# Expert stage of a three-block transformer step: PSUM banks by turns, one bias product for small experts, splits on one engine, another order of experts

## The chip, the cores and the metric

One core of a Trainium2 chip runs the whole program in one launch. The metric is the device time of that launch in microseconds (us); the median of three runs stands for the kernel.

## What is computed

Three transformer blocks follow one another on 512 tokens of width 1024. The change touches only the mixture of experts in the first block. Cut to what matters here:

```python
def moe(h, w_router, b_router, w1, b1, w2, b2):
    logits = xf @ w_router + b_router              # 512 tokens, 32 experts
    top_val, top_idx = lax.top_k(logits, 4)
    gates = jax.nn.softmax(top_val, axis=-1)
    ...
    def expert_block(xb, e):
        u = xb @ w1[e] + b1[e]                     # 1024 -> 2048
        glu = jnp.minimum(u[:, ::2], 7.0)
        lin = jnp.clip(u[:, 1::2], -7.0, 7.0)
        a = glu * jax.nn.sigmoid(1.702 * glu) * (lin + 1.0)
        return a @ w2[e] + b2[e]                   # 1024 -> 1024
    ...                                            # y[token] += gate * row
```

All arrays are 32-bit floats, so each expert has 12 MB of weights, and every expert is used.

## The kernel before

The program is written in a framework that takes instructions in program order, reorders them on each engine by a model of its own, assigns buffers from pools (a tag with `bufs=n` has n slots) and sets the semaphores. Each engine then works through its own queue in that fixed order. An instruction that waits holds up everything behind it on its engine.

Experts are ranked by their number of tokens. Rank 0 is expert F0. Ranks 1 and 2 ("heavy") have one block of 128 slots and one of 64; ranks 3 to 16 ("large") have one block of 128, 96 or 80 slots; ranks 17 to 31 ("small") have one block of 64. Below L9 is the large expert of rank 9, S24 the small one of rank 24, H1 and H2 the heavy ones. Tokens beyond that room would go through a loop at the end (L1410), which makes no pass with these inputs.

Each expert is one call of `expert` (L1228) with three products over 1024 rows, called gemms here: two halves of w1 (`hf` 0 and 1) and w2. A gemm takes four weight units of 1 MB, each with two of the eight k-tiles `kt`.

- **A large block** works in split precision. For each k-tile `wsplit` (L299) makes a rounded high part on ScalarE (L302) and the rest on VectorE (L303), or on GpSimd for the k-tiles that `on_pool` names, which is `kt` 3 of every gemm. Then six products of 512 columns follow (L1260). Three slots exist for each part, and every fourth split takes another pair (`vh`, `vl`).
- **A small block** multiplies the unsplit weights in full 32-bit form. Its two column halves lie in the upper and the lower 64 partitions of one PSUM bank and run side by side.

Each gemm starts with its bias, added by a product of a selector (`sel`) with the table `bias` (L1246). The table's rows come in four groups of 32: high parts and rests of the first 1536 of 3072 columns, then those of the last 1536. A small block needs two such products per gemm, one of them in full 32-bit form; the trace shows three records for the two.

After each half of w1 the gate is computed from PSUM (L1273 to L1277: VectorE, with a tanh on ScalarE), and TensorE transposes the result (L1207) into the operand of w2. After w2 ScalarE scales the rows (L1322, L1325) and GpSimd adds them to the array `yd` in DRAM by an indirect DMA (L1323, L1326). The gather of a block's tokens (L1217, L1221) is a DMA of GpSimd's queue too.

Weight loads are issued by SyncE (L951, L296) into nine `mraw` and two `raw` buffers of 1 MB; a buffer is free again when its last reader is done. PSUM has eight banks: the tag `mm` has two slots of two banks, `s1` two of one bank, `t` two of one bank for transposes.

The order is fixed by hand (L1302 to L1312): F0 S17 L3 S18 L4 S19 L5 S20 L6 S21 H2 L7 S22 L8 S23 L9 S24 L10 S25 L11 H1 S26 L12 S27 L13 S28 L14 S29 L15 S30 L16 S31. Before the last expert, `collect` (L1328) reads `yd` back with four loads on SyncE's queue into two `mraw` buffers. Its eight `add` steps transpose that with TensorE (L1337) and add it to x (L1338); in program order they belong to the last expert's w2 gemm, where `gemm` takes two after each odd k-tile.

Of the kernel before, what the change touches and what calls it, by code (L numbers as in the profile page):

```python
# [11 lines left out]
F32 = mybir.dt.float32  # L12
# [912 lines left out]

N1 = 17
N2 = 2
HEAVY, SKIP = (5, 10), (4, 9)
ROOM = (128,) * 6 + (96,) * 4 + (80,) * 7 + (64,) * 15
OV = 32 + N2  # L930
NB = OV + 15
# [2 lines left out]
def moe(k):  # L934
# [27 lines left out]
    bias = mp.tile([128, 1536], F32R, name="bias")  # L962
    bf = mr.tile([128, 2048], F32, tag="mraw", name="bf", bufs=9)[:, 0:1536]
    for j in range(4):
        o_ = 1536 * (j // 2)
        nc.sync.dma_start(bf[32 * j:32 * j + 32], a["b12"][:, o_:o_ + 1536])
    S.activation(bias, bf, AF.Copy)
    for r_ in (slice(32, 64), slice(96, 128)):
        for c in range(2):
# [25 lines left out]
            S.activation(row[:, cc], ps, AF.Copy, scale=k.rc[:, t:t + 1])  # L995
        G.dma_start(hrow[t * 128:(t + 1) * 128], row, accum_op=ALU.add)
    yield
    k.psum(mm=2, s1=2, t=2)
    ep = es.enter_context(tc.tile_pool(name="ep", bufs=2))
    gd = ep.tile([128, 8, 32], F32, name="gd", bufs=1)  # L1000
    G.memset(gd, 1.0 / D)
# [39 lines left out]
    fl = lambda v: v.rearrange("p e t -> p (e t)")  # L1041
    V.tensor_tensor_scan(fl(Mi), fl(t4), fl(M), 0.0, op0=ALU.mult, op1=ALU.add)

    cnt, pg = (k.pt("s1") for j in range(2))
    nc.tensor.matmul(cnt[0:32, 256:320], Mi[:, :, 3], k.ones[:, 0:64], start=True, stop=True, skip_group_check=True)
    nc.tensor.matmul(cnt[:, 0:128], k.ones, fl(Mi), start=True, stop=True, skip_group_check=True)
    total = cnt[:, 0:128].rearrange("p (e t) -> p e t", t=4)[:, :, 3]
# [177 lines left out]
            X.append(at)  # L1225
        return X

    def expert(w1, w2, blocks, selcol, between=None, on_pool=((3,),) * 3, last=False, drain=False, to=lambda: None):  # L1228

        X = gather(blocks)
        A = [operand("a", False, lambda v, kt: v[:, kt // 4 * 2 + kt % 2, 64 * (kt % 4 // 2):64 * (kt % 4 // 2) + 64]) if b_[0] == 64
             else operand("a", True, lambda v, kt, ns=b_[0]: v[:, kt, 0:ns]) for b_ in blocks]
        split = any(b_[0] > 64 for b_ in blocks)

        def gemm(w, ops, bcol):

            pss = []
            for ns, *_ in blocks:  # L1240
                ps = k.pt("s1").unsqueeze(1) if ns == 64 else k.pt("mm", (128, 2, 512))
                o = [ps[64 * c:64 * c + 64, 0] if ns == 64 else ps[0:ns, c] for c in range(2)]
                for c in range(2):
                    hf, b0 = divmod(bcol + c * 512, 1536)
                    f = (lambda v: v.bitcast(F32)) if ns == 64 and c else (lambda v: v)
                    nc.tensor.matmul(o[c], f(selcol[:, hf]).to_broadcast([128, ns]), f(bias[:, b0:b0 + 512]), start=True, stop=False)  # L1246
                pss.append((ps, o))
            for q in range(4):
                raw = w[q]() if callable(w[q]) else w[q]
                for j in range(2):  # L1250
                    kt = 2 * q + j
                    if between and not last and bcol == 1024 and kt == 4:
                        between[0]()
                    if split:
                        hi, lo = ready.pop(0) if ready else wsplit(raw[:, j], kt in on_pool[bcol // 1024], to())
                    for op_, (_, o) in zip(ops, pss):
                        terms = ((op_[0], hi), (op_[0], lo), (op_[1], hi)) if len(op_) == 2 else ((op_[0], raw[:, j]),)
                        for n_, (l, r_) in enumerate(terms):
                            for c in range(2):
                                nc.tensor.matmul(o[c], l(kt), r_[:, c * 512:(c + 1) * 512], start=False,  # L1260
                                                 stop=kt == 7 and n_ == len(terms) - 1)
                    if adds and kt % 2 and (drain or not split):
                        adds.pop(0)()
                        if adds and not (split and len(blocks) == 1):
                            adds.pop(0)()
            return [ps if b_[0] == 64 else ps[0:b_[0]] for (ps, _), b_ in zip(pss, blocks)]
        for hf in range(2):
            for ps, (a_, _), (ns, *_) in zip(gemm([w1(hf, q) for q in range(4)], X, hf * 1024), A, blocks):
                w, nh = ps.shape[0:2]
                pg, pl = ps[:, :, 0:256], ps[:, :, 256:512]  # L1270
                tl = lambda name, bufs: ep.tile([128, 2, 256], F32, tag=name, name=name, bufs=bufs)[0:w, 0:nh]
                gl, th, ln = tl("gl", 2), tl("gt", 1), tl("ln", 1)
                V.tensor_scalar(gl, pg, 7.0, None, op0=ALU.min)  # L1273
                S.activation(th, gl, AF.Tanh, scale=0.5 * 1.702)  # L1274
                V.tensor_scalar(ln, pl, 7.0, -7.0, op0=ALU.min, op1=ALU.max)
                V.scalar_tensor_tensor(gl, th, 1.0, gl, op0=ALU.add, op1=ALU.mult)
                V.scalar_tensor_tensor(gl, ln, 1.0, gl, op0=ALU.add, op1=ALU.mult)  # L1277
                n = 2 * nh
                to_features([v[:, n * hf:n * hf + n] for v in a_], gl.rearrange("p a b -> p (a b)"), n, w, 0.5)
            if hf and between and not last:  # L1280
                between[1]()
        adds.extend(collected)
        collected.clear()
        pys = gemm([w2(q) for q in range(4)], [a_[1] for a_ in A], 2048)
        while adds and (drain or not split):
            adds.pop(0)()
        for py, (ns, _, tok, gcol, *row) in zip(pys, blocks):
            if not last:
                scatter(py, gcol, row[0], ns)
                continue  # L1290
            rows, *steps = add_rows(py, gcol, tok, ns, last)
            rows()
            adds.extend(steps)
        while last and adds:
            adds.pop(0)()
            if between and len(adds) == 0:
                between()
# [1 line left out]
    def block(b):  # L1299
        return (ROOM + (64,) * N2)[b], tabi[:, b:b + 1] if b else gi0, tab[:, 0, b:b + 1], tab[:, 1, b:b + 1], tabi[:, b:b + 1]  # L1300
    sq = lambda ap: ap.rearrange("o p a f -> p (o a) f")
    small, large = list(range(N1, 32)), list(range(1, N1))  # L1302

    for i_, x_ in zip(HEAVY, reversed(range(1, N2 + 1))):
        large.remove(x_)
        large.insert(i_, x_)
    order = [0, small.pop(0)]
    for i_, x_ in enumerate(large):
        order.append(x_)
        if i_ not in SKIP:  # L1310
            order.append(small.pop(0))
    assert sorted(order) == list(range(32))  # L1312
    k.sg = k.sm.tile([128, T], F32, tag="nwt", name="sg", bufs=1)

    yd, yd2 = k.yd, k.yd.rearrange("t (a b) -> (t a) b", a=2)
# [12 lines left out]
    def collect():  # L1328

        ys = [mr.tile([128, 2, D], F32, tag="mraw", name="yc", bufs=9) for j in range(2)]  # L1330
        for t in range(4):
            nc.sync.dma_start(ys[t // 2][:, t % 2], yd[128 * t:128 * t + 128])

        def add(n):
            ps = k.pt("mm", (128, 2, 512))[:, 0]
            for t in range(4):
                nc.tensor.transpose(ps[:, t * 128:(t + 1) * 128], ys[t // 2][:, t % 2, n * 128:(n + 1) * 128], k.ident)  # L1337
            V.scalar_tensor_tensor(k.x[:, n], ps, mod[:, 40 + n:41 + n], k.x[:, n], op0=ALU.mult, op1=ALU.add)  # L1338
        return [lambda n=n: add(n) for n in range(8)]

    def add_rows(py, gcol, tok, ns, last):
# [27 lines left out]
        def add(n):  # L1369
            if n == 0:  # L1370
                st["P"] = k.sm.tile([128, T], F32R, tag="tmp", name="Pm", bufs=3)
                for t in range(4):
                    V.tensor_scalar(st["P"][:, t * 128:(t + 1) * 128], iota, 1.0 + 128 * t, tok, op0=ALU.add, op1=ALU.is_equal)
            if n % 2 == 0:
                st["ps"] = k.pt("mm", (128, 2, 512))
            ps = st["ps"][:, n % 2]
            for i, (y, r_) in enumerate(st["y"]):
                nc.tensor.matmul(ps, y[r_, 128 * n:128 * n + 128], st["P"][r_], start=i == 0, stop=i == len(st["y"]) - 1)
            if last and st["prev"]:
                sums(*st["prev"])  # L1380
            V.scalar_tensor_tensor(k.x[:, n], ps, mod[:, 40 + n:41 + n], k.x[:, n], op0=ALU.mult, op1=ALU.add)
            if last:
                sq_ = k.sm.tile([128, T], F32, tag="tmp", name="sq", bufs=3)
                S.activation(sq_, k.x[:, n], AF.Square)
                st["prev"] = n, sq_
# [8 lines left out]
    for p in order:  # L1394
        blocks = [block(p)] + ([block(31 + p)] if 1 <= p <= N2 else [])
        if p == 0:
            expert(lambda hf, q: first[4 * hf + q], lambda q: (lambda: wload(a["w2"][0, q])), blocks, sel[:, :, 0:1], (tables, tables2), ((6,), (2, 4, 6), (3,)))
            prev = 0
            continue
        e = nc.values_load(sigi[0:1, p:p + 1], engines=(mybir.EngineType.SP,), min_val=0, max_val=31)  # L1400
        own = p == order[-1]
        drain = own
        prev = p
        if own:
            collected.extend(collect())
        expert(lambda hf, q: (lambda: wload(sq(a["w1"][bass.ds(e, 1), hf, q]), own)),
               lambda q: (lambda: wload(sq(a["w2"][bass.ds(e, 1), q]), own)), blocks, sel[:, :, p:p + 1], last=own, drain=drain,
               between=first_weights if own else None)
    nov = nc.values_load(ovi[0:1, 0:1], min_val=0, max_val=15)
    with tc.For_i(0, nov, 1) as i:  # L1410
# [894 lines left out]
```

## Time and profile before

| | |
|---|---|
| median of 3 runs | 3476.31 us (3474.74 to 3478.86) |
| profiled execution | 3469.57 us |
| its span, first to last instruction | 3467.8 us |
| TensorE busy | 3252.7 us, 94% |
| VectorE busy | 1955.9 us, 56% |
| ScalarE busy | 1337.4 us, 39% |
| GpSimd busy | 536.6 us, 15% |
| mean granted TensorE clock | 0.980 |

Busy shares are means over stages with different limits. PE is TensorE, PEld its weight loads, DVE VectorE, ACT ScalarE, POOL GpSimd, SP SyncE; a name with q is an engine's sequencer. In a row, the text in brackets is how long the engine sat idle before the instruction and what released it. The expert stage lies from 706.6 us to about 2007 us of the span.

### The profile page before, as it was taken

The numbers are of one execution on the slowest core, as the hardware profiler recorded it, in microseconds if no ns is written. First come the engines' busy times: TensorE is split into PE (matmuls) and PEld (weight loads), VectorE is DVE, ScalarE is ACT, GpSimd is POOL, SyncE is SP. The second block draws the span as 40 slices with busy tenths as digits, with TensorE's granted clock in tenths as the row PEclk, the third lists the DMA queues.
The fourth block names the chain that finished last, engine by engine and source line by source line (L and its number), as shares of the span: only waits on it lengthen the run. The fifth ranks groups of instructions, "written<-read, shape, count | busy, mean of one in ns | idle before, by whom it ended". The sixth has DMA issues, their size and how long they took to land. (4 is left out here: it accounts for less than half of the span.)

```text
span 3467.8 us, 41222 instructions
## 1 busy us (share of the span) xinstructions
PE 3252.7 (94%) x15711; PEld 2236.4 (64%) x15711; DVE 1955.9 (56%) x2879; ACT 1337.4 (39%) x1966; POOL 536.6 (15%) x546
## 2 busy tenths in 40 slices
PE   6999999979899998899988799999999999999998
PEld 6779887755554544444444366777777777678876
DVE  7651335474554644574445467765646765555655
ACT  2233344333443533454334245332224533344433
POOL 1223000231211111221112010221111011010001
PEclk9999999989999999999999899999999999999999
DMA  7437223559998799969999511444522210022222
GB/s 264 170 114 249 96 77 126 191 189 391 360 364 310 263 352 361 367 239 343 360 360 356 229 66 52 152 169 158 182 89 100 96 46 4 14 86 97 89 94 85
DMA packets 110425, 668.50 MB, mean 193 GB/s; under 512 B 14416, under 2 KB 14520, under 8 KB 41744
## 3 DMA queue, kind: packets, MB, share of 16 engines
q1 hardware_dynamic: 82272, 575.44, 43.1%
q0 software_dynamic: 27952, 90.38, 9.2%
q8 instruction: 125, 2.05, 0.2%
q14 instruction: 76, 0.62, 0.1%
HBM read 647.56 MB, written 28.63 MB: 195 GB/s over the span
## 5 line engine op out<-in xcount | busy, mean ns | idle before, releaser
L302 ACT ACTIVATE whi<-raw 128x1024 fp32r<-128x1024 f32 x344 | 362.9, 1058 | 664.9 <-PE mm L353 507.4
L303 DVE TENSOR_TENSOR wlo<-raw,whi 128x1024 fp32r<-128x1024 f32 x342 | 422.7, 1239 | 297.8 <-ACT whi L302 290.8
L352 PE MATMUL mm<-h_hi,whi 128*128 128x512 f32 x1440 | 576.4, 400 | 4.7 <-DVE th L637 1.6
L353 PE MATMUL mm<-h_lo,whi 128*128 128x512 f32 x1440 | 575.9, 400 | 0.0
L354 PE MATMUL mm<-h_hi,wlo 128*128 128x512 f32 x1440 | 574.8, 399 | 0.0
L303 DVE TENSOR_TENSOR wlo<-mraw,whi 128x1024 fp32r<-128x1024 f32 x256 | 331.8, 1315 | 114.4 <-ACT whi L302 111.4
L352 PEld LDWEIGHTS mm<-h_hi,whi 128*128 128x128 f32 x1440 | 270.6, 188 | 82.7 <-issue 13.2
L353 PEld LDWEIGHTS mm<-h_lo,whi 128*128 128x128 f32 x1440 | 270.7, 188 | 67.8 <-issue 7.0
L354 PEld LDWEIGHTS mm<-h_hi,wlo 128*128 128x128 f32 x1440 | 270.6, 188 | 67.4 <-issue 5.6
L302 ACT ACTIVATE whi<-mraw 128x1024 fp32r<-128x1024 f32 x258 | 268.7, 1054 | 86.7 <-PE mm L1260 60.6
L1260 PE MATMUL mm<-whi,x 128*80 128x512 f32 (+2 forms) x816 | 244.6, 403 | 0.0
L1260 PE MATMUL s<-mraw,x 128*64 128x512 f32 x888 | 224.7, 599 | 0.0
L1260 PEld LDWEIGHTS mm<-whi,x 128*80 128x80 f32 (+2 forms) x816 | 134.1, 168 | 76.4 <-issue 16.9
L1273 DVE TENSOR_SCALAR gl<-s 128x256 f32<-128x256 f32 x34 | 14.4, 424 | 297.9 <-PE s L1260 297.9
L303 POOL TENSOR_TENSOR ws<-mraw,ws 128x1024 fp32r<-128x1024 f32 x39 | 111.0, 2846 | 329.5 <-ACT ws L302 329.4
L1274 ACT ACTIVATE gt<-gl 128x256 f32<-128x256 f32 (+3 forms) x68 | 35.5, 522 | 300.5 <-DVE gl L1273 294.6
L370 PE MATMUL mm<-whi,h_hi 128*128 128x256 f32 x480 | 138.6, 289 | 3.3 <-DVE rs L601 1.7
L352 PE MATMUL mm<-fhi,whi 128*128 128x512 f32 x352 | 139.4, 396 | 0.0
L353 PE MATMUL mm<-flo,whi 128*128 128x512 f32 x352 | 139.2, 395 | 0.0
L354 PE MATMUL mm<-fhi,wlo 128*128 128x512 f32 x352 | 139.1, 395 | 0.0
L1260 PEld LDWEIGHTS s<-mraw,x 128*64 128x64 f32 x888 | 64.0, 137 | 116.2 <-issue 111.8
L1260 PE MATMUL mm<-wlo,x 128*80 128x512 f32 (+2 forms) x408 | 132.3, 404 | 6.3 <-DVE wlo L303 3.9
(732 smaller groups left out, 5796.4 us busy)
## 6 DMA issues: line engine op xcount, KB each, us to landing
mraw<-in_w_dram SPq DMA_DIRECT2D x316, 1024.0 KB, 8.0
raw<-in_w_dram SPq DMA_DIRECT2D x68, 1024.0 KB, 9.4
mw<-in_wmod_dram POOLq DMA_DIRECT2D x48, 512.0 KB, 4.4
raw<-in_w_dn_dram SPq DMA_DIRECT2D x24, 1024.0 KB, 4.8
raw<-in_w_gu_dram SPq DMA_DIRECT2D x22, 1024.0 KB, 4.9
raw<-in_w_up_dram SPq DMA_DIRECT2D x22, 1024.0 KB, 4.8
mw<-in_wada_dram POOLq DMA_DIRECT2D x32, 512.0 KB, 4.5
raw<-in_w_aqk_dram SPq DMA_DIRECT2D x12, 1024.0 KB, 4.9
```

The costliest lines, as they stand in the source:

```text
L302: nc.scalar.activation(hi, raw, AF.Copy)
L303: ins = (nc.gpsimd if pool_lo else nc.vector).tensor_sub(lo, raw, hi.bitcast(F32))
L352: nc.tensor.matmul(pss[t], hi[:, k, s], xs[0][:, k0 + k], start=first, stop=False)
L353: nc.tensor.matmul(pss[t], hi[:, k, s], xs[1][:, k0 + k], start=False, stop=False)
L354: nc.tensor.matmul(pss[t], lo[:, k, s], xs[0][:, k0 + k], start=False, stop=last)
L370: nc.tensor.matmul(ps, xs[0][:, k, s], hi[:, k % 4], start=k == 0, stop=False)
L1260: nc.tensor.matmul(o[c], l(kt), r_[:, c * 512:(c + 1) * 512], start=False, stop=kt == 7 and n_ == len(terms) - 1)
L1273: V.tensor_scalar(gl, pg, 7.0, None, op0=ALU.min)
L1274: S.activation(th, gl, AF.Tanh, scale=0.5 * 1.702)
```

## The change

Five things are edited, all in the expert stage.

1. **Banks.** The tags `mm` and `s1` with two slots become `mm0`, `mm1`, `s0`, `s1` with one slot each, and `bank` names them by turns in program order.
2. **Bias.** The table is laid out so that both column halves of a gemm stand in the same columns, the first half in partitions 0 to 63 and the second in 64 to 127. A small block builds a 128x128 selector `sw` by one copy on GpSimd per expert, and each gemm then needs one product (fp32r) for both halves. Large blocks keep two products.
3. **Splits.** The default of `on_pool` becomes empty: all rests are made on VectorE, except in F0, which names its own.
4. **Order.** A counter `ahead` chooses the next kind. It gives F0 L3 S17 L4 L5 S18 L6 L7 S19 L8 L9 S20 L10 L11 S21 L12 L13 S22 L14 L15 S23 L16 S24 H1 S25 S26 S27 H2 S28 S29 S30 S31.
5. **Read back.** The four loads of `yd` go to GpSimd's queue. The eight `add` steps are taken two at a time after k-tiles 4 to 7 of the last w2 gemm, and their transposes are tied on TensorE behind the last product of k-tile 3.

```diff
-HEAVY, SKIP = (5, 10), (4, 9)
...
     for j in range(4):
-        o_ = 1536 * (j // 2)
-        nc.sync.dma_start(bf[32 * j:32 * j + 32], a["b12"][:, o_:o_ + 1536])
+        nc.sync.dma_start(bf[32 * j:32 * j + 32].rearrange("e (j f) -> e j f", f=512),
+                          a["b12"].rearrange("e (j c f) -> e c j f", c=2, f=512)[:, j // 2])
...
-    k.psum(mm=2, s1=2, t=2)
+    k.psum(mm0=1, mm1=1, s0=1, s1=1, t=2)
+    turn = {"mm": 0, "s": 0}
+
+    def bank(name, *shape):
+
+        turn[name] ^= 1
+        return k.pt(f"{name}{turn[name]}", *shape)
...
-    def expert(w1, w2, blocks, selcol, between=None, on_pool=((3,),) * 3, last=False, drain=False, to=lambda: None):
+    def expert(w1, w2, blocks, selcol, between=None, on_pool=((),) * 3, last=False, to=lambda: None):
...
+        if blocks[-1][0] == 64:
+            sw = ep.tile([128, 128], F32R, tag="sw", name="sw")
+            G.tensor_copy(sw.rearrange("p (c s) -> p c s", c=2), selcol.to_broadcast([128, 2, 64]))
...
-                ps = k.pt("s1").unsqueeze(1) if ns == 64 else k.pt("mm", (128, 2, 512))
+                ps = bank("s").unsqueeze(1) if ns == 64 else bank("mm", (128, 2, 512))
                 o = [ps[64 * c:64 * c + 64, 0] if ns == 64 else ps[0:ns, c] for c in range(2)]
-                for c in range(2):
-                    hf, b0 = divmod(bcol + c * 512, 1536)
-                    f = (lambda v: v.bitcast(F32)) if ns == 64 and c else (lambda v: v)
-                    nc.tensor.matmul(o[c], f(selcol[:, hf]).to_broadcast([128, ns]), f(bias[:, b0:b0 + 512]), start=True, stop=False)
+                b_ = bias[:, bcol // 2:bcol // 2 + 512]
+                if ns == 64:
+                    nc.tensor.matmul(ps[:, 0], sw, b_, start=True, stop=False)
+                else:
+                    for c in range(2):
+                        nc.tensor.matmul(o[c], selcol[:, c].to_broadcast([128, ns]), b_, start=True, stop=False)
...
-                    if adds and kt % 2 and (drain or not split):
-                        adds.pop(0)()
-                        if adds and not (split and len(blocks) == 1):
+                    if kt == 3:
+                        turn["half"] = ins.ins
+                    for _ in range(2 if kt > 3 else 0):
+                        if adds:
                             adds.pop(0)()
...
-        while adds and (drain or not split):
-            adds.pop(0)()
...
+    kinds = {"small": list(range(N1, 32)), "large": list(range(N2 + 1, N1)), "heavy": list(range(1, N2 + 1))}
+    order, ahead = [0], 0
+    while any(kinds.values()):
+        want = ("small", "large", "heavy") if ahead > 0 else ("large", "small", "heavy") if ahead > -3 else ("heavy", "large", "small")
+        if len(kinds["small"]) == 1:
+            want = ("large", "heavy", "small")
+        kind = next(n for n in want if kinds[n])
+        order.append(kinds[kind].pop(0))
+        ahead += {"small": -4, "large": 2, "heavy": 11}[kind]
...
         for t in range(4):
-            nc.sync.dma_start(ys[t // 2][:, t % 2], yd[128 * t:128 * t + 128])
+            G.dma_start(ys[t // 2][:, t % 2], yd[128 * t:128 * t + 128])
 
         def add(n):
-            ps = k.pt("mm", (128, 2, 512))[:, 0]
-            for t in range(4):
-                nc.tensor.transpose(ps[:, t * 128:(t + 1) * 128], ys[t // 2][:, t % 2, n * 128:(n + 1) * 128], k.ident)
+            ps = bank("mm", (128, 2, 512))[:, 0]
+            with tc.issue_after(turn["half"]):
+                for t in range(4):
+                    nc.tensor.transpose(ps[:, t * 128:(t + 1) * 128], ys[t // 2][:, t % 2, n * 128:(n + 1) * 128], k.ident)
```

## Rows read from the trace of the kernel before

**Rows 1.** Busy time of engines by stretch: experts two to 31, S31, tail.

```profile
core 0: us, PE busy (x) PEld busy (x) DVE busy (x) ACT busy (x) POOL busy (x), PEclk, DMA share, GB/s
773.70:1943.10 1169.40, 1074.04 (x4474) 545.21 (x4472) 641.44 (x658) 499.84 (x595) 218.97 (x111) 0.98 0.87 332
1943.10:1991.00 47.90, 32.66 (x136) 12.79 (x135) 10.26 (x17) 4.11 (x7) 1.43 (x1) 0.82 0.91 358
```

**Rows 2.** Groups by line, TensorE, 773.7 to 1943.1: busy, mean ns | idle before.

```profile
L1246 PE MATMUL s<-bias,sel 128*64 128x512 f32 x150 | 71.5, 555 | 26.6 <-DVE ln L1275 18.0 <-ACT yr L1322 8.7
L1207 PE MATMUL t<-ident,gl 128*128 128x128 f32 (+2 forms) x192 | 32.0, 276 | 48.4 <-DVE gl L1277 48.4
L1246 PE MATMUL mm<-bias,sel 128*80 128x512 f32 (+2 forms) x96 | 31.3, 410 | 10.5 <-ACT yr L1325 10.5
```

**Rows 3.** Waits of TensorE, 773.7 to 1991: us in total, times, longest.

```profile
PE mm L1337 <- DMA yc<-yd: 12.4, 4, 9.6
...
PE s L1260 <- DMA mraw<-in_w_dram: 0.6, 1, 0.6
```

**Rows 4.** Timeline around the gate of L14: start, us, engine, instruction, idle before.

```profile
1764.66 0.68 DVE L1276 SCALAR_TENSOR_TENSOR gl<-gt,gl 80x512 f32<-80x512 f32 x1
1765.65 3.05 POOL L303 TENSOR_TENSOR ws<-mraw,ws 128x1024 fp32r<-128x1024 f32 x1 [10.15 <-ACT ws L302]
1766.40 2.84 DVE L1277 SCALAR_TENSOR_TENSOR gl<-ln,gl 80x512 f32<-80x512 f32 x1
1769.30 0.50 PE L1207 MATMUL t<-ident,gl 80*128 80x80 f32 x4 [1.85 <-DVE gl L1277]
```

**Rows 5.** Timeline of TensorE after the gate before w2 of L14.

```profile
1786.85 1.05 PE L1260 MATMUL mm<-whi,a 128*80 128x512 f32 x2
...
1791.52 0.61 PE L1260 MATMUL mm<-whi,a 128*80 128x512 f32 x2
```

**Rows 6.** Busy time by stretch (columns of rows 1): L14, then S29.

```profile
1748.81:1794.73 45.92, 40.23 (x163) 23.32 (x164) 36.05 (x31) 27.02 (x30) 11.34 (x5) 0.96 0.92 352
1794.73:1823.56 28.83, 26.16 (x116) 8.40 (x116) 4.10 (x10) 3.54 (x9) 2.78 (x3) 1.00 0.94 349
```

**Rows 7.** Split on VectorE by form, 1662 to 1943: busy, mean ns | idle before.

```profile
L303 DVE TENSOR_TENSOR wlo<-raw,whi 128x1024 fp32r<-128x1024 f32 x14 | 16.8, 1214 | 1.8 <-ACT whi L302 1.8
```

**Rows 8.** Timeline of TensorE: bias products in S29, and two gemms' together before S22.

```profile
1803.38 0.98 PE L1246 MATMUL s<-bias,sel 128*64 128x512 f32 x2 [0.95 <-DVE ln L1275]
...
1208.68 2.85 PE L1246 MATMUL s<-bias,sel 128*64 128x512 f32 x6
1211.46 1.17 PE L1246 MATMUL mm<-bias,sel 128*96 128x512 f32 x4
```

**Rows 9.** Timeline from the end of L16: read back of yd, transposes, S31 begins.

```profile
1949.38 1.75 SPq L1332 DMA_DIRECT2D yc<-yd  x4
...
1952.71 0.66 PE L1337 MATMUL mm<-ident,yc 128*128 128x128 f32 x2 [9.56 <-DMA yc<-yd]
...
1961.92 2.12 PE L1260 MATMUL s<-mraw,x 128*64 128x512 f32 x8
...
1963.97 1.09 PE L1337 MATMUL mm<-ident,yc 128*128 128x128 f32 x8
```

**Rows 10.** Weight queue, 1600 to 1700: packets, MB; then engines 1100 to 1200.

```profile
q1 hardware_dynamic: 5328, 38.80, 94.9%
...
1100.00:1200.00 100.00, 97.79 (x389) 52.18 (x389) 68.00 (x67) 56.29 (x62) 21.23 (x10) 1.00 0.73 265
```

**Rows 11.** The scatter of a small block: ns min/median/max; its landing.

```profile
L1323 POOL DMA_INDIRECT yd<-yr,tabi x16: 1554/1562/2179, 804.0 to 1898.6; - x16
...
DMA to landing us min/median/max: 9.0/9.1/11.9
```

**Rows 12.** GpSimd's gathers of small blocks, and its splits, 774 to 1943.

```profile
L1217 POOL DMA_INDIRECT xg<-hrow,tabi x17: 1014/1074/1091, 759.9 to 1868.7; - x17
...
L303 POOL TENSOR_TENSOR ws<-mraw,ws x37: 2364/3047/3207, 830.4 to 1929.8; 128x1024 fp32r<-128x1024 f32 x37
```

More of the change, by code (lines that the diff above doesn't have):

```diff
@@ L1042, in moe @@
     V.tensor_tensor_scan(fl(Mi), fl(t4), fl(M), 0.0, op0=ALU.mult, op1=ALU.add)
-    cnt, pg = (k.pt("s1") for j in range(2))
+    cnt, pg = (bank("s") for j in range(2))
     nc.tensor.matmul(cnt[0:32, 256:320], Mi[:, :, 3], k.ones[:, 0:64], start=True, stop=True, skip_group_check=True)
@@ L1259, in gemm @@
                             for c in range(2):
-                                nc.tensor.matmul(o[c], l(kt), r_[:, c * 512:(c + 1) * 512], start=False,
-                                                 stop=kt == 7 and n_ == len(terms) - 1)
-                    if adds and kt % 2 and (drain or not split):
-                        adds.pop(0)()
-                        if adds and not (split and len(blocks) == 1):
+                                ins = nc.tensor.matmul(o[c], l(kt), r_[:, c * 512:(c + 1) * 512], start=False,
+                                                       stop=kt == 7 and n_ == len(terms) - 1)
+                    if kt == 3:
+                        turn["half"] = ins.ins
+                    for _ in range(2 if kt > 3 else 0):
+                        if adds:
                             adds.pop(0)()
@@ L1301, in moe @@
     sq = lambda ap: ap.rearrange("o p a f -> p (o a) f")
[L1302 to L1312, printed above, removed]
+    kinds = {"small": list(range(N1, 32)), "large": list(range(N2 + 1, N1)), "heavy": list(range(1, N2 + 1))}
[7 more added lines that the diff above has]
+        ahead += {"small": -4, "large": 2, "heavy": 11}[kind]
+    assert sorted(order) == list(range(32)) and order[-1] >= N1
     k.sg = k.sm.tile([128, T], F32, tag="nwt", name="sg", bufs=1)
@@ L1374, in add @@
             if n % 2 == 0:
-                st["ps"] = k.pt("mm", (128, 2, 512))
+                st["ps"] = bank("mm", (128, 2, 512))
             ps = st["ps"][:, n % 2]
@@ L1397, in moe @@
             expert(lambda hf, q: first[4 * hf + q], lambda q: (lambda: wload(a["w2"][0, q])), blocks, sel[:, :, 0:1], (tables, tables2), ((6,), (2, 4, 6), (3,)))
-            prev = 0
             continue
@@ L1401, in moe @@
         own = p == order[-1]
-        drain = own
-        prev = p
         if own:
@@ L1406, in moe @@
         expert(lambda hf, q: (lambda: wload(sq(a["w1"][bass.ds(e, 1), hf, q]), own)),
-               lambda q: (lambda: wload(sq(a["w2"][bass.ds(e, 1), q]), own)), blocks, sel[:, :, p:p + 1], last=own, drain=drain,
+               lambda q: (lambda: wload(sq(a["w2"][bass.ds(e, 1), q]), own)), blocks, sel[:, :, p:p + 1], last=own,
                between=first_weights if own else None)
```

## The prediction

> **What bounds the kernel now.** I read the busy time by stretch first. From the end of F0 (773.7) to the end of L16 (1943.1) there are 1169.4 us: TensorE is busy in 1074, VectorE in 641, the DMA engines in 0.87 of it [rows 1]. So TensorE leads and the weight transfers come second. Are the weights ever late? The waits of TensorE say no: 0.6 us in all [rows 3]. TensorE is therefore held by its own work and by gaps between its products.
>
> The groups by line say where the 1169.4 - 1074.0 = 95.4 us of idle time lie: 48.4 before the transposes of the gate, waiting for L1277; 26.6 before small bias products; 10.5 before large ones [rows 2]. That is 85.5 of 95.4. The rest is spread over late splits.
>
> The timeline shows why the first wait is long. In L14, L1277 takes 2.84 us where its neighbour L1276, of the same form and size, takes 0.68; it ends 0.5 us after a GpSimd split that runs from 1765.65 to 1768.70. TensorE stands still for 1.85 us and then transposes [rows 4]. After the second such stop the same pair of products takes 1.05 us, and 0.61 a few us later [rows 5]: the granted clock of L14 is 0.96, with 1.00 in S29 [rows 6], so part of it ran at the lower of the two levels (1.2 instead of 2.4 GHz).
>
> One more thing is read from order. The bias product at 1803.38 waits for the reader of the bank that the previous gemm used [rows 8]. The two banks do alternate: before S22 six records, two gemms' bias, stand together without a wait [rows 8]. So at 1803.38 the queue holds the bias of a later gemm, pulled forward to the moment when its bank should come free, ahead of products that could run.
>
> **The change part by part.** The sum is made against the profiled execution, 3469.57 us, of which 1.8 lie outside the span of 3467.8; the median of the runs is 6.7 us higher, so what is saved is taken off 3476.3 at the end.
>
> Splits leave GpSimd. Three for each of the 16 large and heavy experts make 48; 37 of them stand in one row with a median of 3.05 us [rows 12]. VectorE does one in 1.21 us [rows 7]. In L14 it gains 3 x 1.21 = 3.6 us of work and loses two stretches of L1277, 2 x (2.84 - 0.68) = 4.3. VectorE goes from 36.05 us [rows 6] to about 35.4 in an expert that will take TensorE about 39 (45.9 less two stops of 1.85, the clock's 1.8 below and one wait for a bank). That is 91%: loaded, but not the bound. The wait of 48.4 us [rows 2] should mostly go. What is late next is the split itself, so I take 40 (20 to 48).
>
> The clock follows. In L14 a granted 0.96 of 45.92 us is a loss of 0.04 x 45.92 = 1.8 us [rows 6]. Eleven large experts look like it, 20 us. I take 12 (0 to 20), since other stops remain.
>
> Bias of small blocks: 50 gemms in this stretch have 71.5 us of busy time, 1.43 each [rows 2], and 2.85 / 2 = 1.43 where nothing overlaps [rows 8]. In steady state part of it runs beside the first half's products; 0.98 is the stretch of the first two records [rows 8]. The new product is of the form of the large block's bias, four of which take 1.17 us, and one alone 0.41 [rows 8, 2]. So 51 gemms save at least 51 x (0.98 - 0.41) = 29 and at most 51 x (1.43 - 0.29) = 58; TensorE leads, so nearly all of it counts. I take 38 (26 to 55).
>
> `sw` costs one GpSimd copy per expert. The trace has none of this size. A split there takes 3.05 us [rows 12] and has eight times the elements, so between 0.4 and 3.05; GpSimd is busy 219 of 1169 us [rows 1] and loses 48 splits, so I charge nothing while it runs ahead (else see the last rival). Laying out the table happens before F0, beside loads, at nothing.
>
> Banks by turns: 26.6 + 10.5 = 37.1 us hang on this [rows 2]. The banks already alternate, so turns alone free nothing; what would is another place of the bias in the queue, and the planner sets that anew. I take 18 (0 to 37).
>
> Order: a large expert that follows a small one starts cold, its first splits not yet made. No row shows that start alone. L14 is idle for 45.92 - 40.23 = 5.7 us [rows 6], 3.7 of it in the two stops, so a start costs between 0 and 2.0. Such starts become fewer, 9 instead of 15. I take 5 (0 to 12). A large expert behind a large one has no small one before it in which VectorE splits ahead; that is inside the bound of the first part.
>
> The weights get tighter. At best 38.80 MB pass in 100 us [rows 10], a unit of 1.049 MB in 2.70 us, an expert in 32.4. The pair L14 and S29 takes 45.92 + 28.83 = 74.75 us and needs 64.8 of transfer [rows 6]. With all the terms above a pair would fall by 2 x 1.85 + 1.8 + 2 x 0.95 + 3 x 0.7 + 1 = 10.5 to about 64, which is what the transfers allow. In a heavy expert TensorE needs twice that, the eleven buffers are full, and the DMA share falls to 0.73 [rows 10]; the new order puts three and four small experts behind one to use that lead: 11 units x 2.70 = 30 us, against the lead that a small expert spends: 32.4 less its new 24.8 (28.8 less two stops of 0.95 [rows 8] and 3 x 0.7 for the bias), 7.6. Three spend 23, four 30. It just holds. I charge 10 us lost for late weights (0 to 40).
>
> Read back: TensorE stands from 1943.1 to 1952.7 and creeps on to 1961.9, waiting for loads that follow the last scatter [rows 9]; S31 takes 47.9 us [rows 1] against 28.8 of S29 [rows 6]. The 32 transposes stay, 8 in 1.09 us [rows 9], so 4.4. That leaves 47.9 - 28.8 - 4.4 = 14.7. I take 13 (-9 to 16). They move behind k-tile 3 of the last w2, some 20 us later. On SyncE the weights of S31 no longer stand behind the four loads. On GpSimd the loads wait for S30's scatter, which lands after 9.1 us [rows 11]; behind them only the gather of S31 could stand, and then the 9 us are lost once.
>
> The sum: 40 + 12 + 38 + 18 + 5 - 10 + 13 = 116. The profiled time would be 3469.6 - 116 = 3354 and the median 3476.3 - 116 = **3360 us**. All ends upward give 48 + 20 + 55 + 37 + 12 + 0 + 16 = 188, 3288; all downward 20 + 0 + 26 + 0 + 0 - 40 - 9 = -3, 3479.
>
> **The rivals.** *Everything goes, and the weights take over.* For: no wait for weights now, and every gap has a named cause. Against: the pair's 64.8 us. From 773.7, 372 units less 11 loaded ahead are 361 x 2.70 = 975 us; the two heavy experts leave about 62 us of transfer time unused (0.27 of 100 us in rows 10, somewhat more around H1). So the last w2 ends near 773.7 + 1037 + 8 = 1819 instead of 1991: 172 less, 3304.
>
> *The stalls only change place.* VectorE at 91% in one order of splits and gates is late for the transposes all the same, and the planner keeps pulling the bias forward. For: the planner's order is rebuilt and does not know of the stretched operations. Against: those stretches end with the GpSimd splits. Then the low ends of the first four parts hold: 20 + 0 + 26 + 0 + 5 - 10 = 41, 3435.
>
> *Slower: GpSimd's queue becomes the bound for small experts.* Each small bias needs `sw`. If its copy stands behind the scatter of the expert before, TensorE waits for the issue (1.56 [rows 11]) and the copy (0.4), 2.0 us. If that scatter first waits for the landing of the one before, 9.1 more [rows 11]: 11.1 x 15 = 167 us, 51 more than the sum saves: 3527. It decides from 116 / 15 = 7.7 us per small expert. Against: `sw` hangs on nothing but the selector and its own buffer, of which there are two, so it can be issued an expert ahead, as the gathers are.
>
> [...]
>
> **How the numbers follow.** The forecast holds 0.56 (3320 to 3400), weights taking over 0.15, stalls changing place 0.18 (3400 to 3469), no net effect 0.03, the slower rival 0.08. The two other gains reach into the range until no more than a fifth is left out: 3295 to 3445. About 0.2% (7 us) is what a measurement of this kernel can tell from no change; faster by more than that has 0.56 + 0.15 + 0.18 = 0.89, within it 0.03, slower 0.08.
>
> **What would show it.** Right: no GpSimd split after F0; L1277 at 0.68 us in large experts and idle before L1207 under 15 us; one record per small gemm at L1246 of about 0.4 us; the granted clock of large experts near 1.00; S31 under 36 us without a stop before L1337; a DMA share above 0.92. Wrong: TensorE waiting for weights by more than 40 us; idle before L1246 as long as now, which would show that the planner and not the tags set it; idle before L1246 released by GpSimd. The forecast falls if VectorE is busy for 95% of a large expert, or if two large experts in a row take over 90 us.

## The result and the profile after

The kernel after takes 3391.1 us (median of four runs, 3387.8 to 3397.0), the kernel before 3475.5 us beside it. The ratio is 0.976 with a 95% interval of 0.9742 to 0.9778: 84 us saved, where 116 were forecast. The time lies inside the range on record, but several terms of the sum behind it do not hold. The profiled execution has a span of 3389.1 us.

Busy time by stretch, kernel after (columns as in rows 1): the experts from the end of F0 to the middle of S30, one large expert (L14), S31, and the tail of the stage.

```profile
core 0: us, PE busy (x) PEld busy (x) DVE busy (x) ACT busy (x) POOL busy (x), PEclk, DMA share, GB/s
779.50:1846.30 1066.80, 1018.67 (x4330) 533.14 (x4330) 602.81 (x701) 495.74 (x587) 91.28 (x78) 1.00 0.94 360
1375.40:1416.20 40.80, 38.91 (x166) 23.68 (x167) 35.87 (x37) 28.70 (x33) 1.78 (x2) 0.96 0.97 365
1858.50:1909.30 50.80, 32.14 (x127) 10.62 (x127) 10.98 (x17) 5.24 (x8) 3.81 (x5) 0.83 0.91 354
1909.30:1928.00 18.70, 14.27 (x34) 3.71 (x32) 8.78 (x13) 6.78 (x11) 0.00 (x0) 0.82 0.00 0
```

Against [rows 1] the granted clock of the experts is 1.00 in place of 0.98, the DMA share 0.94 in place of 0.87, and GpSimd is busy for 91 us in place of 219. Read from one expert's first main product to the next's, L14 takes 40.8 us, where it took 45.1 by the same cut before; [rows 6] start at the bias products and have 45.9. It follows a small expert and still has a granted clock of 0.96; L15 behind it takes 38.4 at 1.00. All fourteen large experts (L3 to L16) take 38.7 us on average. L16 had the read back in its cut before; the thirteen others fell from 44.2 to 38.7, 71 us together. A small expert in steady state (S19 to S23) takes 29.3 us, and S29 took 29.6 by this cut before. So nearly the whole gain lies in the large experts.

Waits of TensorE, kernel after, 779.5 to 1935 (us in total, times, longest):

```profile
PE s L1252 <- DVE ln L1285: 20.8, 22, 1.0
PE s L1269 <- DMA mraw<-in_w_dram: 15.9, 3, 13.3
PE s L1252 <- ACT yr L1330: 8.7, 11, 0.8
PE mm L1255 <- ACT yr L1333: 8.6, 11, 0.9
PE mm L1269 <- DVE wlo L303: 7.6, 28, 0.6
PE t L1502 <- DMA lv<-in_lamv_dram: 5.3, 1, 5.3
...
PE t L1212 <- DVE gl L1287: 0.3, 1, 0.3
```

The wait for the gate, 48.4 us in [rows 2], is down to 0.3. The waits before the bias products (L1252 small, L1255 large) are as long as before: 20.8 + 8.7 + 8.6 = 38.1 us against 26.6 + 10.5 = 37.1. A wait for weights is new, 13.3 of its 15.9 us in one place, the start of S31.

Timeline of TensorE, kernel after: the start of the second gemm of a small expert, S21.

```profile
1245.88 0.47 PE L1252 MATMUL s<-bias,sw 128*128 128x512 f32 x1 [0.95 <-DVE ln L1285]
1246.28 1.07 PE L1269 MATMUL s<-raw,x 128*64 128x512 f32 x2
1247.28 0.44 PE L1212 MATMUL t<-ident,gl 128*128 128x128 f32 x2
1247.65 1.50 PE L1269 MATMUL s<-raw,x 128*64 128x512 f32 x5
```

The bias is one record of 0.47 us, as forecast, and it still waits 0.95 us for the reader of the bank. From its start to the main products behind the transposes it is 1247.65 - 1245.88 = 1.77 us. In the kernel before, the bias of [rows 8] at 1803.38 goes on like this:

```profile
1804.20 0.59 PE L1246 MATMUL s<-bias,sel 128*64 128x512 f32 x1
1804.20 0.59 PE L1260 MATMUL s<-mraw,x 128*64 128x512 f32 x1
1804.73 0.44 PE L1207 MATMUL t<-ident,gl 128*128 128x128 f32 x2
1805.10 7.08 PE L1260 MATMUL s<-mraw,x 128*64 128x512 f32 x30
```

The last of its records runs beside a main product, and the same stretch lasts 1805.10 - 1803.38 = 1.72 us. So the shorter bias gains nothing here.

### The profile page after: what moved, and what is told of

The parts are those of the page before. It is cut to its first block, busy times and chain, and to the rows that moved or that the text cites. A ratio compares the mean times of both kernels' runs of the same rounds, so it can differ in the third digit from the quotient of the medians.

```text
span 3389.1 us, 41014 instructions
## 1 busy us (share of the span) xinstructions
PE 3209.7 (95%) x15609; PEld 2225.9 (66%) x15609; DVE 1923.5 (57%) x2927; ACT 1339.0 (40%) x1966; POOL 415.5 (12%) x519
## 5 line engine op out<-in xcount | busy, mean ns | idle before, releaser
L302 ACT ACTIVATE whi<-raw 128x1024 fp32r<-128x1024 f32 x354 | 373.8, 1059 | 661.1 <-PE mm L353 497.5
L303 DVE TENSOR_TENSOR wlo<-raw,whi 128x1024 fp32r<-128x1024 f32 x352 | 435.2, 1239 | 312.2 <-ACT whi L302 305.4
L303 DVE TENSOR_TENSOR wlo<-mraw,whi 128x1024 fp32r<-128x1024 f32 x246 | 295.3, 1218 | 75.0 <-ACT whi L302 73.0
L302 ACT ACTIVATE whi<-mraw 128x1024 fp32r<-128x1024 f32 x248 | 258.6, 1056 | 92.2 <-PE mm L1269 73.7
L1269 PE MATMUL s<-mraw,x 128*64 128x512 f32 x896 | 234.8, 606 | 16.0 <-DMA mraw<-in_w_dram 15.9
L371 PE MATMUL mm<-wlo,h_hi 128*128 128x256 f32 x480 | 136.0, 283 | 2.1 <-DVE wlo L303 2.0
```

What stands on the lines that cost most here:

```text
L302: nc.scalar.activation(hi, raw, AF.Copy)
L303: ins = (nc.gpsimd if pool_lo else nc.vector).tensor_sub(lo, raw, hi.bitcast(F32))
L371: nc.tensor.matmul(ps, xs[0][:, k, s], lo[:, k % 4], start=False, stop=False)
L1269: ins = nc.tensor.matmul(o[c], l(kt), r_[:, c * 512:(c + 1) * 512], start=False, stop=kt == 7 and n_ == len(terms) - 1)
```

## The experiments

Two theories were set against each other. One is the sum on record, each term by itself. The other (called P or A in the expectations below) says that the splits carry nearly the whole result, and that the bias products wait because the planner puts them too early in TensorE's queue, so that neither their bank nor their length decides. Every ratio is against the kernel before on the same chip.

**The splits alone.** The kernel before with this one edit:

```diff
-    def expert(w1, w2, blocks, selcol, between=None, on_pool=((3,),) * 3, last=False, drain=False, to=lambda: None):
+    def expert(w1, w2, blocks, selcol, between=None, on_pool=((),) * 3, last=False, drain=False, to=lambda: None):
```

> The kernel before with one edit: no split on GpSimd after the first expert. Theory A (this one edit carries nearly the whole result, because the gate of each large expert no longer stops TensorE and VectorE and ScalarE take the splits in their slack): 3395 to 3410 us, ratio 0.977 to 0.981, large experts at some 39 us each, the idle before the gate's transposes under 2 us in place of 48.4. Theory of the sum on record (this term is 40 us and the clock 12, the rest comes from the other edits): 3423 us, ratio 0.985. If the waits only change place (rival 'stalls only change place'): over 3435 us.

Measured: 3394.1 us, ratio 0.9786 (0.9768 to 0.9804), 77 us. One line of the change makes nearly the whole result. Order of experts and program are otherwise those of before, so the stretches compare one to one. Busy time by stretch of this kernel (columns as in rows 1), the experts two to 31 (773.7 to 1943.1 before) and L14 from first main product to the next expert's:

```profile
775.30:1866.80 1091.50, 1048.24 (x4473) 535.95 (x4471) 607.84 (x706) 499.63 (x595) 85.36 (x63) 1.00 0.92 355
1692.40:1731.40 39.00, 37.36 (x165) 22.62 (x164) 32.68 (x34) 26.12 (x29) 1.51 (x2) 1.00 0.99 389
```

The same cut of L14 in the kernel before:

```profile
1750.20:1795.30 45.10, 39.41 (x163) 23.19 (x162) 35.58 (x31) 26.07 (x29) 10.44 (x5) 0.96 0.90 350
```

The stage falls by 1169.4 - 1091.5 = 77.9 us. Idle time of TensorE goes from 95.4 [rows 1] to 43.3, 52.1 less; busy time falls by 1074.0 - 1048.2 = 25.8 with the same products, at a granted clock of 1.00 in place of 0.98. The granted clock of single experts before, here L8, L10 and H1, says how much of that the clock is:

```profile
1240.00:1286.30 46.30, 40.95 (x165) 26.68 (x165) 31.92 (x29) 23.95 (x27) 10.38 (x6) 0.93 0.89 347
1390.90:1434.60 43.70, 37.95 (x165) 22.41 (x164) 35.52 (x31) 26.07 (x29) 10.55 (x6) 1.00 0.92 359
1509.30:1581.40 72.10, 71.10 (x274) 33.54 (x273) 39.28 (x39) 29.75 (x35) 12.94 (x7) 1.00 0.54 182
```

Ten large experts were below 1.00 (L6 and L8 at 0.93, the others at 0.96); L3, L7, L10, L12 and both heavy ones were at 1.00, though L10 has two stops of TensorE as well. What the ten lost, time by time, adds up to some 20 us, and with the splits gone nothing is below 1.00. So about a quarter of the gain is products that no longer run at the lower clock after a stop; the other 5 us of the busy time aren't assigned. VectorE took over the splits and is still busy for less time (35.58 to 32.68 in L14), since its two-input operations no longer stretch: the gate's, and in part its own splits (1315 ns on average over the whole program before, 1218 in the kernel after, in the group wlo<-mraw).

**The splits back.** The reverse edit in the kernel after:

> The kernel after with one edit undone: kt 3 of every gemm of 80 to 128 rows is split on GpSimd again. Theory A: 60 to 80 us lost, 3450 to 3470 us, ratio 0.993 to 0.999, the gate's two-input products on VectorE at 2 to 3 us again and the idle before the gate's transposes at 40 us or more. Theory of the sum: 40 to 52 us lost, 3430 to 3443 us, ratio 0.988 to 0.991.

Measured: 3462.7 us, ratio 0.9975 (0.9964 to 0.9986). All the rest of the change together is worth 9 us. The first wait of TensorE in this kernel:

```profile
PE t L1212 <- DVE gl L1287: 49.8, 33, 1.9
```

and all of its L1287 (ns min/median/max, first and last start):

```profile
L1287 DVE SCALAR_TENSOR_TENSOR gl<-ln,gl x68: 415/678/2876, 741.7 to 1965.7; 128x256 f32<-128x256 f32 x34, 80x512 f32<-80x512 f32 x14, 128x512 f32<-128x512 f32 x12, 96x512 f32<-96x512 f32 x8
```

The same line in the kernel after has 687 ns at most:

```profile
L1287 DVE SCALAR_TENSOR_TENSOR gl<-ln,gl x68: 415/552/687, 746.6 to 1897.9; 128x256 f32<-128x256 f32 x34, 80x512 f32<-80x512 f32 x14, 128x512 f32<-128x512 f32 x12, 96x512 f32<-96x512 f32 x8
```

So the stretched product goes and comes back with the GpSimd splits, and the wait of TensorE with it. The Trainium skill (SBUF — State Buffer, section "SBUF: two separate sides") says that a VectorE operation with two inputs in SBUF and a GpSimd operation that reads SBUF lock each other out for the whole instruction. [Rows 4] agree: the split ends at 1768.70, and 0.68 us more is 1769.38; L1277 ended at 1769.24.

**Banks.** Two buffers of one name in place of explicit turns:

```diff
-    k.psum(mm0=1, mm1=1, s0=1, s1=1, t=2)
+    k.psum(mm=2, s=2, t=2)
...
-        turn[name] ^= 1
-        return k.pt(f"{name}{turn[name]}", *shape)
+        return k.pt(name, *shape)
```

> The changed kernel with the bank tags undone: mm and s with two slots each, chosen by the planner. Theory P: the two banks alternate without explicit turns, so nothing changes, 3391 within 8 us (the planner moves other stages by a few us whenever anything is edited), and the waits before bias products stay at 29 and 9 us. Rival B (the turns are what keeps the banks apart and let the large experts fall to 38.7 us): 20 us or more slower, waits before bias products up by that much.

Measured: 3395.1 us, ratio 0.9783 (0.9759 to 0.9807), not to be told from the kernel after. The three waits before bias products are 20.8, 8.7 and 8.6 us here too. Turns by hand change nothing.

**The bias in its two products** (second one in plain f32, as before), without `sw`:

```diff
-                    nc.tensor.matmul(ps[:, 0], sw, b_, start=True, stop=False)
+                    for c in range(2):
+                        f = (lambda v: v.bitcast(F32)) if c else (lambda v: v)
+                        nc.tensor.matmul(o[c], f(selcol[:, c]).to_broadcast([128, ns]), f(b_), start=True, stop=False)
```

> The changed kernel with two bias products per gemm of a small block again (one fp32r, one full 32-bit, three records), the selector copy on GpSimd left out, the new table kept. The step of the prediction's sum says 38 us (26 to 55) slower. Theory P says the old pair ran beside the first half's products and the single product leaves those products alone instead, so in steady state nothing is gained: 0 to 12 us slower, all of it in the few small experts whose products stand in program order (S17 and those behind a heavy expert).

Measured: 3405.6 us, ratio 0.9815 (0.9798 to 0.9831); the profiled span is 14 us longer than that of the kernel after, the time by the ratios 19. So one product is worth 14 to 19 us: half of the 38 of the sum, and more than the 12 at most of theory P. Its place is where P had it: the two heavy experts hold 5.7 (73.6 and 71.9 us here, 70.0 and 69.8 after), L3 and S17 together 5.3, the small ones behind the heavy ones (S25, S28) 3.4, and a small expert in steady state takes 29.6 against 29.3. The large experts from L4 on are 6.4 us shorter here than in the kernel after; three of them that have a granted clock of 0.96 there (L8, L12, L14) are at 1.00 here.

**The bias behind the gemm before it.** The kernel after, with each bias product tied behind the last main product of the preceding gemm:

```diff
+                with (tc.issue_after(turn["last"]) if turn.get("last") else ExitStack()):
                     if ns == 64:
                         nc.tensor.matmul(ps[:, 0], sw, b_, start=True, stop=False)
...
+            turn["last"] = ins.ins
```

> The changed kernel with one edit: each bias product is tied on TensorE behind the last product of the gemm before it, so the planner cannot pull it forward. Theory P (the planner's queue order costs the small experts their gain, not the bank tags): the waits of TensorE before the small and large bias products, 29.5 and 8.6 us in the changed kernel, go to under 5 us; a small expert in steady state falls from 29.3 us to 26 to 27.5, since part of the time reappears before the transposes of the gate; 20 to 40 us faster than the changed kernel, 3351 to 3371. Rival D (the small experts run at the rate of the weights): the waits only move to the weights, small experts stay near 29 us, the time stays within 6 us of 3391.

Measured: 3374.9 us, ratio 0.9719 (0.9701 to 0.9737), by the ratios 14 us less than the kernel after, where 20 to 40 were forecast; a small expert in steady state takes 28.5 us, above the forecast of 26 to 27.5. The waits of 38.1 us are gone; that is what shows that the place in the queue made them. Waits of TensorE in this kernel, 779 to 1920:

```profile
PE s L1270 <- DMA mraw<-in_w_dram: 18.6, 4, 14.6
PE t L1212 <- DVE gl L1289: 13.1, 24, 1.7
PE s L1270 <- ACT x L1204: 8.5, 10, 1.1
```

Part of them comes back one place further on: the gate's transposes are pulled forward in the same way, to two products behind the bias, and now wait themselves (13.1 us).

**Old order.** The kernel after with small and large experts in turn, the list of before:

> The kernel after with the old order of the experts (small and large in turn, a heavy one in the middle and one later). The sum on record gave the order 5 us (0 to 12), so 3396 us, ratio 0.977 (0.976 to 0.980). Rival, the weights: in the old order a large expert follows each small one, so TensorE leaves the loads more slack and each small expert finds its weights there; then waits for mraw fall from 15.9 us to under 5 and the time falls by up to 12 us: 3379 us, ratio 0.972.

Measured: 3392.9 us, ratio 0.9775 (0.9757 to 0.9793). The forecast of 5 us fits the difference of the ratios (0.0015), but it can't be told from nothing. (The sum counted 15 starts behind a small expert in the old list; there are 14.) The rival fell: the wait for mraw stays (16.8 us, the longest 14.3).

**The last expert's weights first.** In the kernel after, the first loads of the following stage (w_qk, w_v) are tied behind S31's own:

```diff
-        nc.sync.dma_start(raw, src)
+        own_load[:] = [nc.sync.dma_start(raw, src).ins]
...
-        k.pre = {(id(w), u): k.wunit(w, u) for u in range(3)}
+        with tc.issue_after(own_load[0]):
+            k.pre = {(id(w), u): k.wunit(w, u) for u in range(3)}
```

> The changed kernel with one edit: the two loads of the next block's first weights are tied on SyncE behind the last weight load of S31. Theory W (S31 starts 14.6 us late because its own weights stand behind the next block's loads in SyncE's queue, which wait for buffers, not because of the read back): the 13.3 us wait of TensorE for the first weights of S31 goes to under 3 us and S31 takes 30 to 36 us instead of 50.8; 12 to 20 us faster than the changed kernel, about 3375. Rival (four small experts in a row have used up the transfer lead, so the weights would be late in any order): the wait stays above 8 us, time within 5 us of 3391.

Why: the timeline of the kernel after shows SyncE's queue in front of S31, and TensorE's stop.

```profile
1846.28 10.88 SPq L296 DMA_DIRECT2D raw<-in_w_qk_dram  x2
1862.60 0.33 SPq L296 DMA_DIRECT2D raw<-in_w_v_dram  x1
1863.13 28.21 SPq L950 DMA_DIRECT2D mraw<-in_w_dram  x12
...
1873.09 3.68 PE L1269 MATMUL s<-mraw,x 128*64 128x512 f32 x8 [13.30 <-DMA mraw<-in_w_dram]
```

Measured: 3381.6 us, ratio 0.9743 (0.9726 to 0.9759). The wait for the weights goes from 13.3 us to 0.2, so theory W has the cause right. S30 and S31 together take 66.4 us in place of 78.3; in that TensorE now waits 5.9 us for yc, and F0 begins 2.2 us later, so that the time falls by only 6 us by the ratios, 8 by the spans, where 12 to 20 were forecast.

**Read back as it was.** The kernel after with the loads of yd on SyncE and the transposes from the first k-tiles on:

```diff
-            G.dma_start(ys[t // 2][:, t % 2], yd[128 * t:128 * t + 128])
+            nc.sync.dma_start(ys[t // 2][:, t % 2], yd[128 * t:128 * t + 128])
...
-            with tc.issue_after(turn["half"]):
-                for t in range(4):
...
-                    for _ in range(2 if kt > 3 else 0):
+                    for _ in range(2 if kt % 2 else 0):
```

> The kernel after with the read back as it was: the four loads of yd on SyncE and the 32 transposes in any part of the last expert, without the tie behind k-tile 3 of the last w2. The sum on record gave this term 13 us: 3404 us, ratio 0.980, with TensorE stopped some 10 us before the transposes on top of the 13.3 us before the last expert's weights. Rival, second cover: the weights of S31 and the read back arrive in the same stretch, so the stop for yc takes the place of the stop for mraw and the last expert takes 48 to 52 us as in both kernels: 3388 to 3395 us, ratio 0.975 to 0.977.

Measured: 3386.9 us, ratio 0.9762 (0.9736 to 0.9788): no difference from the kernel after. Waits of TensorE in this kernel:

```profile
PE s L1252 <- DVE ln L1285: 20.8, 22, 1.0
PE mm L1345 <- DMA yc<-yd: 10.8, 4, 7.8
```

There is no wait for S31's weights now: the two stops cover each other, as the second theory said, and S30 with S31 takes 75.0 us against 78.3. So the new read back gains nothing; by this stretch it is 3 us longer.

**Both, and a step more.** The bias in order and S31's weights first, together:

> The kernel after with both edits that made it faster alone: each bias product behind the last product of the gemm before it (alone 0.9719), and the next stage's first weights behind the last expert's own loads (alone 0.9743). If the two gains lie in different places, as the segments of the two runs say (14 us in the large and small experts, 7 in the last one): 3367 us, ratio 0.970. If they share a limit (the loads): 3375 us, ratio 0.972.

Measured: 3364.5 us, ratio 0.9699 (0.968 to 0.9718); the gains add. Then, on top, the gate's transposes of small blocks tied behind the second k-tile of the next gemm:

```diff
+                    if kt == 1:
+                        while turn["feat"]:
+                            turn["feat"].pop(0)(ins.ins)
...
-                to_features([v[:, n * hf:n * hf + n] for v in a_], gl.rearrange("p a b -> p (a b)"), n, w, 0.5)
+                if ns == 64:
+                    turn["feat"].append(feat)
+                else:
+                    feat()
```

(`feat` is the same call, with its transposes under issue_after.)

> The run with bias products in order and own weights first, and with the gate's transposes of every small block tied behind the second k-tile of the gemm that follows (two of the four main groups before the first use). The 11.0 us before the gate's transposes should go; the bound is 11 us less, 3353 us, ratio 0.967. Rival, the loads: the DMA engines are at 0.95 of that stretch, so waits for mraw (4.7 us now) take the place of it: 3360 to 3365 us, ratio 0.969 to 0.970.

Measured: 3338.8 us, ratio 0.962 (0.9595 to 0.9645). This is faster than both kernels, and 26 us better than the step before it, where 11 were taken for the bound. A steady small expert falls from 28.5 to 25.7 us. By the profiled executions (27 us) 20 lie between the first products of F0 and S31, 4 ahead of F0, where nothing was edited, and 3 behind. Timeline of TensorE, the second gemm of S20 in the step before (transposes after two products):

```profile
1132.30 0.50 PE L1254 MATMUL s<-bias,sw 128*128 128x512 f32 x1
1132.73 1.07 PE L1271 MATMUL s<-mraw,x 128*64 128x512 f32 x2
1134.36 0.41 PE L1213 MATMUL t<-ident,gl 128*128 128x128 f32 x2 [0.55 <-DVE gl L1290]
1134.70 4.94 PE L1271 MATMUL s<-mraw,x 128*64 128x512 f32 x21
...
1141.71 0.51 PE L1254 MATMUL s<-bias,sw 128*128 128x512 f32 x1
```

and the same gemm with the transposes after eight:

```profile
1124.25 0.49 PE L1255 MATMUL s<-bias,sw 128*128 128x512 f32 x1
1124.68 1.94 PE L1272 MATMUL s<-mraw,x 128*64 128x512 f32 x8
1126.54 0.44 PE L1214 MATMUL t<-ident,gl 128*128 128x128 f32 x2
1126.91 3.65 PE L1272 MATMUL s<-mraw,x 128*64 128x512 f32 x16
...
1132.21 0.50 PE L1255 MATMUL s<-bias,sw 128*128 128x512 f32 x1
```

From bias to bias it is 9.41 us and 7.96. Only 0.55 of the 1.45 us between them was booked as a wait. The two halves of a small block's output run side by side in a stream: sixteen products take 3.65 us, 0.23 each, while two by themselves take 1.07. A stream cut after two products loses 1.07 - 0.46 = 0.61 us, one cut after eight 1.94 - 1.82 = 0.12. That explains another 0.5; the last 0.4 of the gemm isn't assigned. With this the loads come into view: DMA share 0.96 over the experts, and 22 waits for mraw with 15.8 us in all, where the step before had five with 4.7.

## Why the prediction was right, and where it was not

| Term of the sum | taken | measured | from |
|---|---|---|---|
| splits off GpSimd, idle time | 40 | 52 | splits alone |
| clock of the large experts | 12 | 26, some 20 of it the clock | splits alone, busy time |
| one bias product | 38 | 14 to 19 | two bias products |
| banks by turns | 18 | 0 | two buffers of one name |
| order | 5 | 0 to 5 | old order |
| late weights, S31 left out | -10 | -3 | 15.9 - 13.3 of the waits |
| read back | 13 | 0 | read back as it was |
| F0 and the tail of the stage | none | -12 | below |

With the middles the measured terms make about 52 + 26 + 16 + 2 - 3 - 12 = 81 of 84 us. They come from different kernels, so a few us are within their doubt. Against the 116 of the sum, splits, clock and late weights did some 33 us better and all the rest 68 worse. That the time lay 32 us off, and not 68, is a cancelling of errors: luck, as far as the sum goes. What the prediction had right is the cause of the largest term.

*Splits: right in mechanism, too small in size.* The prediction read the cause from [rows 4] and [rows 5] and named it as the largest term. All but 0.3 of the 48.4 us went, above the 40 it took, because the feared successor, a late split, grew by little: the waits for wlo are 7.6 us, where they were 4.8, and those for whi 2.7. VectorE is busy for 88% of L14 (35.87 of 40.80), where 91% was forecast.

*Clock: right in mechanism, at the top of its range.* The bound of 20 us was built from eleven large experts at 1.8 us each. Ten were slowed, two of them twice, and without the splits these 20 us came back in full. The 12 left room for stops that remain: in the whole change L8, L12 and L14 still run at 0.96, which costs 5 us again.

*Bias product: the failed step.* The sum priced a record, 0.98 us to 0.41, and held that nearly all of it counts since TensorE leads. The record did shrink. But part of the old bias ran beside a main product (1804.20 above), and in the kernel after the first two main products run alone instead, ahead of the transposes. What counts is the stretch from bias to the stream behind the transposes, 1.72 and 1.77 us. The experiment with two bias products found most of the gain elsewhere: in the heavy experts, in S17, and behind the heavy ones.

*Banks: the failed step was the price of a hope.* The text itself said that turns free nothing and that the queue's place sets the wait, and then took 18 of 37 us because the planner would set it anew. It set it as before; the sign that was named for that ("idle before L1246 as long as now") is what the profile shows. Tying the bias in the queue took these waits away at once.

*Read back: the second cover was not looked for.* The stop behind L16 had two causes that ended close together: the yd loads, and S31's own weights. Those stand on SyncE behind a load of the next stage as well as behind the four yd loads, as its queue in the kernel before shows:

```profile
1942.63 0.33 SPq L296 DMA_DIRECT2D raw<-in_w_v_dram  x1
1949.38 1.75 SPq L1332 DMA_DIRECT2D yc<-yd  x4
1951.33 18.43 SPq L951 DMA_DIRECT2D mraw<-in_w_dram  x12
```

The profile names only the yd loads as releasers of TensorE, from 1952.71 [rows 9] to 1957.59. The first of S31's loads landed after 10.3 us, at 1961.6, and S31's first product comes at 1961.92. With the first cause gone, the second stops TensorE for 13.3 us. "S31 under 36 us" failed (50.8 in the cut of the first table); the 32 transposes in the second half of w2 came as forecast, in four groups of eight at 1.09 us.

*Not in the sum at all.* The first main product of F0 begins at 725.8 in place of 720.3, and the next stage's first transposes begin 23.2 us after the end of the experts in place of 16.3 (from 1991.0 to 2007.27, and from 1909.3 to 1932.49). That is 12 us; F0 itself is 2 us shorter (57.5 to 55.4). Of the second, some 4 us are products at the lower clock: the tail runs at 0.82 after S31's stop, where before it ran at 1.00 (columns as in rows 1):

```profile
1991.00:2006.00 15.00, 10.74 (x24) 2.44 (x24) 7.32 (x10) 6.79 (x11) 0.00 (x0) 1.00 0.00 1
```

The other 3 us are the wait at L1502. The profile names different releasers for it (bd in the kernel before; lv, bt or h_hi in runs where it lasts over 5 us), so its cause stays open.

*Rivals.* "The stalls only change place" was half right: it held for the bias and the read back, not for the gate. "The weights take over" did not come with this change: TensorE waits 15.9 us for weights, 13.3 of them in the one place where another stage's loads stood in front. Its first signs are those of the last experiment. The slower rival did not occur: `sw` costs GpSimd 0.44 us in the median, inside the bounds, and no wait of TensorE for it is on the list.

*Signs.* Of those that were named for being right, S31 under 36 us failed, and the granted clock of 1.00 held but for three large experts. Of those for being wrong, the idle time before the bias came.

## What to carry to other kernels

When an engine's operation is many times longer than its neighbour of the same form, look for another engine's operation that ends with it, and price the removal with the idle time and the slow products behind each stop. A record's duration is not its price: measure from the point where the stream stops to where it is whole again, and before taking a stall away look at what is queued behind the same point. Where a planner orders an engine's queue, a free bank does not move an instruction; tie the instruction to the one it should follow, and then look at the next instruction that was pulled forward.

## What the runs showed beyond this

Edits inside the expert stage moved work ahead of it. The first main product of F0 begins between 717.8 us (read back as it was) and 728.0 (own weights first) over the edits of the kernel after, though neither of these two touches what stands before it. That the planner, which orders all of these instructions, moves them is likely, but no run shows it. So a difference of some 5 us between two kernels says nothing about the edit unless the stretch that it touches is compared by itself.

The stop of TensorE in front of S31 costs more than its 13.3 us, for the granted clock is 0.83 in the stretch with it and still 0.82 in the tail behind it. The kernel before has the first of these too (0.82 in the second of [rows 1]), but not the second. In the tail the same pair of products L1376 takes 1.92 us at first and 1.05 later:

```profile
1914.34 1.92 PE L1376 MATMUL t<-sq,gd 128*32 128x512 f32 x2
...
1923.16 1.05 PE L1376 MATMUL t<-sq,gd 128*32 128x512 f32 x2 [0.54 <-ACT sq L1393]
```
